# A hybrid SSD/MLA/PEER block on one core: the first norm's statistics taken together, roots on ScalarE, and three U chunks held back

## The chip, the core and the metric

The kernel runs on one core of a Trainium2 chip. A core has five engines that run on their own and wait for each other through semaphores: TensorE (matmuls and transposes, into PSUM), VectorE, ScalarE (activations), GpSimd and SyncE, which here only issues transfers. In profiles they are PE, PEld (PE's weight loads), DVE, ACT, POOL and SP. The metric is device microseconds for one execution. Before the change the median of three runs is 1629.04 us (1628.74 to 1629.06).

## The reference

The input `x` has 512 tokens of 1024 values. What matters here:

```
h   = layer_norm(x, ln_in_g, ln_in_b)                       # the first norm
mix = hybrid_mixer(h, ...)                                  # SSD heads, MLA heads, one output projection
h   = layer_norm(alpha * h + mix, ln_mix_g, ln_mix_b)
ffn = peer(h, w_query, sub_keys, u_table, v_table)          # 8 heads, top 16 of 16384 experts each
out = layer_norm(alpha * h + ffn, ln_ffn_g, ln_ffn_b)       # the last norm

def layer_norm(x, g, b):
    mu  = mean(x);  var = mean((x - mu)**2)
    return (x - mu) * rsqrt(var + 1e-5) * g + b
```

In `peer`, expert e of a token adds g_e * v_e * gelu(u_e . x). All arithmetic is in float32.

## The kernel before

The 512 tokens are four blocks of 128 (`NB` = 4). A float32 matmul is made of three matmuls on split operands (`mm3`, lines 71 to 74): high by high, high by low, low by high. The low part of a weight is its raw value minus its high part. All large weights pass through one stream of 128 x 1024 items (`Stream`, lines 79 to 127): SyncE loads an item into one of three raw buffers (`wir`), ScalarE makes the high part (`wih`, or `wihx` for every fourth item; line 109), VectorE or GpSimd the low part (`wil`, line 119). `get(n)` makes the splits up to item n + `la`, the high parts `ha` items beyond these, and after each split asks for the load that takes the freed raw buffer.

The order of work is written out by hand: each engine runs its instructions in the order in which the program issues them, and so does each transfer queue. In one place, while PEER's routing is prepared, a loop (`drive`, line 1248) weighs planned times of TensorE (`tm[0]`) against those of VectorE (`tm[1]`) and puts in a U chunk whenever TensorE's plan is not ahead.

The parts that the change touches:

First norm (lines 260 to 302). SyncE loads the four blocks of `x` into `XH`, then constants and the first weights. VectorE takes mean and variance of blocks 0 and 1 (`bn_stats`, `bn_aggr`), computes the inverse roots with a bit trick and three Newton steps (`rsqrt`, lines 129 to 139), and ScalarE normalises both blocks. TensorE transposes them, eight pieces each, into eight PSUM banks `PS8`; bank k holds piece k of all four blocks. The same follows for blocks 2 and 3, with the normalising shared by VectorE and ScalarE. Then, per k, ScalarE applies gain and bias (`ht`, and for odd k `HH`), VectorE rounds for even k (`HH`) and makes the low part `HL`. The first two column groups of the input projection (`two`) consume them k by k.

PEER sweeps all experts densely for blocks 0 to 2 (but for the last 16 tokens of block 2) and gathers rows for block 3 and those 16. A U chunk (`u_chunk`) is 24 matmuls for 128 experts over 368 tokens and a Gelu into an `act` tile. `build_g` (line 1097) makes the gate matrix in 48 groups: VectorE builds one-hot matrices (`hot`, lines 1109, 1113, 1114), TensorE multiplies them (lines 1132, 1133), ScalarE copies the result into `stg` (line 1135), and after every fourth group SyncE writes `stg` to memory (lines 1139, 1140). U chunks are put between the groups by `drive` up to `LEAD - RES` = 54 - 2 of them; the other two run after `build_g`. Then SyncE reads the gates back (`gt`, line 1300), VectorE multiplies them with `act` (`P`, line 1323), ScalarE and VectorE split the product (`Ph`, `Pl`, lines 1336, 1343), and from there one U chunk and one V chunk alternate (`v_chunk`, lines 1352 to 1356), until all 128 of each are done; the first of these U chunks still precedes V chunk 0.

Last norm (`ln_out`, line 1472). For each of blocks 0 to 2, VectorE adds the residual, takes the statistics, computes the root in small steps (`norm_chain`, lines 141 to 156) and applies the norm in two halves. Block 2 comes last; its centring (line 1492) is interleaved with the small steps of its root, and its second half is sent out by ScalarE's queue.

Of the kernel before, what the change touches and what calls it, by code (L numbers as in the profile page):

```python
# [11 lines left out]
F32 = mybir.dt.float32  # L12
# [12 lines left out]
D = 1024  # L25
NB = 4
# [9 lines left out]
RES = 2  # L36
# [17 lines left out]
def tile_block(ctx: ExitStack, tc: tile.TileContext, I, out):  # L54
# [85 lines left out]

    def norm_chain(p, mv, tag, out):
# [32 lines left out]

    cs2 = pool("cs2", side="right")
# [84 lines left out]
    V.memset(ones, 1.0)  # L260
    mv4 = lnp.tile([128, NB, 2], F32, name="mv4")
    PS8 = [pa() if k < 4 else pb() for k in range(8)]
    for p in range(2):
        bs = slice(2 * p, 2 * p + 2)
        for b in (2 * p, 2 * p + 1):
            st6 = lnp.tile([128, 2, 6], F32, name="st6", bufs=2)
            for i in range(2):
                V.bn_stats(st6[:, i], XH[:, b, i * 512:(i + 1) * 512])
            V.bn_aggr(mv4[:, b], st6.rearrange("p a b -> p (a b)"))
        ve = lnp.tile([128, 2], F32, name="ve", bufs=2)  # L270
        nm = lnp.tile([128, 2], F32, name="nm", bufs=2)
        V.tensor_scalar(ve, mv4[:, bs, 1], EPS, None, op0=OP.add)
        rs = rsqrt(lnp, ve, [128, 2], "l0")
        V.scalar_tensor_tensor(nm, mv4[:, bs, 0], -1.0, rs, op0=OP.mult, op1=OP.mult)
        for j, cs, act in (((0, slice(0, D), 1), (1, slice(0, D), 1)) if p == 0 else
                           ((0, slice(0, D), 0), (1, slice(0, 512), 1), (1, slice(512, D), 0))):
            t = XH[:, 2 * p + j, cs]
            if act:
                A.activation(t, t, AF.Identity, bias=nm[:, j:j + 1], scale=rs[:, j:j + 1])
            else:  # L280
                V.tensor_scalar(t, t, rs[:, j:j + 1], nm[:, j:j + 1], op0=OP.mult, op1=OP.add)
        for k in range(8):
            for b in (2 * p, 2 * p + 1):
                T.transpose(PS8[k][:, b * 128:(b + 1) * 128], XH[:, b, k * 128:(k + 1) * 128], ident)
        if p == 0:
            win.his(2)
# [1184 lines left out]
    def ln_out(b):  # L1471
# [15 lines left out]
        ch = norm_chain(fin, mv, "lf", o)  # L1487
        for i, _ in enumerate(ch):
            yield
            if b == 2 and i in (2, 4):  # L1490
                cs = ce[i // 2 - 1]
                V.scalar_tensor_tensor(t[:, cs], t[:, cs], mv[:, 0:1], R2[:, 0, cs], op0=OP.subtract, op1=OP.mult)
                yield
# [105 lines left out]
```

## Time and profile before

| | |
|---|---|
| median of three runs | 1629.04 us |
| the profiled execution, its own time | 1627.28 us |
| its span in the profile | 1625.5 us |
| TensorE busy | 1582.6 us, 97% of the span |
| VectorE busy | 1377.3 us, 85% |
| ScalarE busy | 699.8 us, 43% |
| GpSimd busy | 463.3 us, 29% |
| moved by transfers | 393.77 MB, 242 GB/s in the mean |

The profile is one execution seen by the hardware. Its page gives the busy time of each engine, the chain of work that ended last (followed back from the last instruction, at each step to what released it), and the costliest groups of instructions. The trace behind it can be asked for a timeline: one row per instruction or run of equal ones, with its start, its length (of the whole run, if there are several), engine, line, what it writes and reads, and in brackets how long the engine had been idle and what ended that. SPq and ACTq are transfers at the time of their issue. A table of stretches gives busy times, the granted TensorE clock (1.00 is full speed) and the transfer rate of chosen stretches. Matmuls are pipelined: the length of one includes its way through the array, and the spacing of the starts is the pace.

### The profile page before, as it was taken

The page shows a single profiled execution, that of the slowest core. Times are in us where ns is not written, and L with a number is a line of the kernel's source. Part 1 is how long each engine was busy: PE and PEld are TensorE (multiplying, and loading weights), DVE is VectorE, ACT ScalarE, POOL GpSimd, SP SyncE. Part 2 cuts the span into 40 slices and gives each one's busy share as a digit, 9 for nine tenths or more (in the row PEclk, how much of TensorE's full clock was granted, in tenths as well). Part 3 has the DMA queues.
Part 4 walks back from the last instruction along what each step waited for, and adds up shares of the span by engine and source line. Part 5 has one row for each costly group of instructions (what it writes and reads, how often), then busy time and mean ns, then how long its engine had stood idle before and what let it go on. Part 6 is the DMA issues. An engine that isn't in the chain of part 4 may idle for free.

```text
span 1625.5 us, 23770 instructions
## 1 busy us (share of the span) xinstructions
PE 1582.6 (97%) x8640; PEld 1394.3 (86%) x8640; DVE 1377.3 (85%) x2649; ACT 699.8 (43%) x1213; POOL 463.3 (29%) x332
## 2 busy tenths in 40 slices
PE   7999999999999999999899999999999999999997
PEld 5777878888888999998899999999999999888886
DVE  8979688947799999999588788788888888988977
ACT  5575466641433545555433333343333333333341
POOL 0000000000143213200155455555554544533300
PEclk9999999999999999999999999999999999999999
DMA  6242121374432458766799999999999999999973
GB/s 245 91 157 91 46 64 47 103 242 143 135 92 86 123 182 292 285 240 244 251 375 345 339 331 354 344 338 343 329 355 337 344 329 352 360 335 342 335 220 122
DMA packets 150604, 393.77 MB, mean 242 GB/s; under 512 B 12536, under 2 KB 64584, under 8 KB 148696
## 3 DMA queue, kind: packets, MB, share of 16 engines
q1 hardware_dynamic: 107400, 237.76, 43.3%
q0 software_dynamic: 42944, 154.24, 26.2%
q8 instruction: 67, 1.10, 0.3%
q14 instruction: 49, 0.40, 0.1%
q10 hardware_dynamic: 144, 0.26, 0.0%
HBM read 359.66 MB, written 31.51 MB: 241 GB/s over the span
## 4 chain that ended last, share of the span: by engine, by line
PE 74%; DVE 21%; ACT 2%; issue 2%; DMA 1%; DVEq 0%; ACTq 0%; SPq 0%
PE va L1352 10%; PE va L1356 10%; PE va L1353 10%; PE pu L72 8%; PE pu L74 8%; PE pu L73 8%; PE pa L74 3%; PE pa L73 3%; PE pa L72 3%; DVE wil L119 3%; DVE ij L1109 3%; DVE g L1113 2%; DVE t L953 1%; PE pw L73 1%; PE pw L74 1%
## 5 line engine op out<-in xcount | busy, mean ns | idle before, releaser
L109 ACT ACTIVATE wih<-wir 128x1024 fp32r<-128x1024 f32 (+2 forms) x269 | 277.9, 1034 | 264.5 <-DMA wir<-v 90.5
L119 DVE TENSOR_TENSOR wil<-wir,wih 128x1024 fp32r<-128x1024 f32 (+1 forms) x254 | 302.2, 1190 | 103.2 <-ACT wih L109 43.0
L74 PE MATMUL pu<-XTH,wil 128*128 128x368 f32 x1008 | 331.9, 329 | 0.7 <-DVE wil L119 0.7
L72 PE MATMUL pu<-XTH,wih 128*128 128x368 f32 x904 | 299.3, 331 | 0.0
L73 PE MATMUL pu<-XTL,wih 128*128 128x368 f32 x904 | 297.0, 329 | 0.0
L1353 PE MATMUL va<-wil,Ph 128*128 128x512 f32 x726 | 282.7, 389 | 0.0
L1389 POOL DMA_INDIRECT row<-u,ix x128 | 187.6, 1465 | 230.1 <-DVE row L1400 136.7
L1389 POOL DMA_INDIRECT row<-v,ix x128 | 181.3, 1416 | 196.0 <-DVE ac L1406 167.6
L74 PEld LDWEIGHTS pu<-XTH,wil 128*128 128x128 f32 x1008 | 189.3, 188 | 1.3 <-DVE wil L119 1.3
L73 PEld LDWEIGHTS pu<-XTL,wih 128*128 128x128 f32 x904 | 170.0, 188 | 2.9
L72 PEld LDWEIGHTS pu<-XTH,wih 128*128 128x128 f32 x904 | 169.8, 188 | 2.9
L1352 PE MATMUL va<-wih,Ph 128*128 128x512 f32 x432 | 168.5, 390 | 0.0
L1406 DVE SCALAR_TENSOR_TENSOR ac<-row,hd,ac 128x1024 f32<-128x1024 f32 x128 | 164.0, 1281 | 3.0 <-DMA row<-v,ix 0.9
L1353 PEld LDWEIGHTS va<-wil,Ph 128*128 128x128 f32 x726 | 136.3, 188 | 25.9
L1205 ACT ACTIVATE act<-pu 128x368 f32<-128x368 f32 x126 | 59.9, 476 | 221.3 <-PE pu L74 196.3
L1400 DVE SCALAR_TENSOR_TENSOR row<-row,x 128x1024 f32<-128x1024 f32 x128 | 150.1, 1219 | 2.4 <-DMA row<-u,ix 2.4
L109 ACT ACTIVATE wihx<-wir 128x1024 fp32r<-128x1024 f32 x67 | 71.1, 1061 | 158.3 <-DMA wir<-v 129.9
L1356 PE MATMUL va<-wih,Pl 128*128 128x512 f32 x432 | 133.4, 390 | 0.0
L119 DVE TENSOR_TENSOR wil<-wir,wihx 128x1024 fp32r<-128x1024 f32 x62 | 75.9, 1223 | 51.4 <-issue 45.5
L1352 PE MATMUL va<-wihx,Ph 128*128 128x512 f32 x294 | 114.9, 391 | 0.9 <-ACT Ph L1336 0.9
L1356 PEld LDWEIGHTS va<-wih,Pl 128*128 128x128 f32 x432 | 81.1, 188 | 17.2
L1352 PEld LDWEIGHTS va<-wih,Ph 128*128 128x128 f32 x432 | 81.2, 188 | 15.8
(458 smaller groups left out, 3073.7 us busy)
## 6 DMA issues: line engine op xcount, KB each, us to landing
wir<-ut SPq DMA_DIRECT2D x128, 512.0 KB
wir<-v SPq DMA_DIRECT2D x128, 512.0 KB
gsp<-stg SPq DMA_DIRECT2D x12, 1920.0 KB
gt<-gsp SPq DMA_DIRECT2D x30, 768.0 KB
wir<-wo SPq DMA_DIRECT2D x26, 512.0 KB
wir<-wf SPq DMA_DIRECT2D x18, 512.0 KB
wir<-wqr SPq DMA_DIRECT2D x16, 512.0 KB
de<-acd POOLq DMA_DIRECT2D x8, 512.0 KB
```

The costliest lines, as they stand in the source:

```text
L72: T.matmul(ps, lh, rh, start=start, stop=False)
L73: T.matmul(ps, lh, rl, start=False, stop=False)
L74: T.matmul(ps, ll, rh, start=False, stop=stop)
L109: A.activation(h, r, AF.Copy)
L119: self.lo(n).tensor_tensor(l, r, h, op=OP.subtract)
L1205: A.activation(ACT[c][:, :NU], ps, AF.Gelu)
L1352: T.matmul(va[b][e], Ph[:, bs], h[:, cs], start=c == 0, stop=False)
L1353: T.matmul(va[b][e], Ph[:, bs], l[:, cs], start=False, stop=False)
L1356: T.matmul(va[b][e], Pl[:, bs], h[:, cs], start=False, stop=c == 127)
L1389: G.indirect_dma_start(out=R[s], out_offset=None, in_=I["u"] if s < 128 else I["v"], in_offset=bass.IndirectOffsetOnAxis(ap=ix[:, s % 128: ...
L1400: V.scalar_tensor_tensor(r, r, 1.0, x3, op0=OP.mult, op1=OP.mult, accum_out=hd[:, s:s + 1])
L1406: V.scalar_tensor_tensor(ac, r, hd[:, s - 128:s - 127], ac, op0=OP.mult, op1=OP.add)
```

## The change

Three edits.

First norm: the statistics of all four blocks come first, then one chain for all four inverse roots (`sqrt_rs`): ScalarE takes the square root of variance + eps, VectorE its reciprocal and one Newton step. ScalarE normalises block 2, VectorE blocks 0, 1 and 3. The transposes follow in the order 0, 2, 1, 3, and the first two high parts of weights (`win.his(2)`) come after them in the program. A one-element root (`w0`) stands at the start, so that ScalarE's table with the root is loaded there.

Last norm: block 2 uses `sqrt_chain`, the same root in five instructions, with the two centring products between them; blocks 0 and 1 keep `norm_chain`. Two one-element activations before the norm make ScalarE load the table of the root.

U chunks: `RES` is 3, so that `drive` stops one U chunk earlier and three run after `build_g`.

```
-RES = 2
+RES = 3
...
+    def sqrt_rs(p, v, shape, tag):
+        h, q, y, a = (p.tile(shape, F32, name=tag + n) for n in "hqya")
+        A.activation(q, v, AF.Sqrt, bias=eps)
+        V.tensor_scalar(h, v, EPS, -0.5, op0=OP.add, op1=OP.mult)
+        V.reciprocal(y, q)
+        V.tensor_tensor(a, y, y, op=OP.mult)
+        V.tensor_tensor(a, a, h, op=OP.mult)
+        V.scalar_tensor_tensor(y, a, 1.5, y, op0=OP.add, op1=OP.mult)
+        return y
+
+    def sqrt_chain(p, mv, tag, out):
+        h, q, a, y = (p.tile([128, 1], F32, name=tag + n) for n in "hqay")
+        A.activation(q, mv[:, 1:2], AF.Sqrt, bias=eps)
+        V.tensor_scalar(h, mv[:, 1:2], EPS, -0.5, op0=OP.add, op1=OP.mult)
+        yield
+        V.reciprocal(y, q)
+        yield
+        V.scalar_tensor_tensor(a, y, h, y, op0=OP.mult, op1=OP.mult)
+        yield
+        V.scalar_tensor_tensor(y, a, 1.5, y, op0=OP.add, op1=OP.mult)
+        out.append(y)
+        yield
...
     V.memset(ones, 1.0)
+    V.memset(eps, EPS)
     mv4 = lnp.tile([128, NB, 2], F32, name="mv4")
+    w0 = lnp.tile([128, 1], F32, name="w0")
+    A.activation(w0, ones[:, 0:1], AF.Sqrt, bias=eps)
     PS8 = [pa() if k < 4 else pb() for k in range(8)]
-    for p in range(2):
-        bs = slice(2 * p, 2 * p + 2)
-        for b in (2 * p, 2 * p + 1):
-            st6 = lnp.tile([128, 2, 6], F32, name="st6", bufs=2)
-            for i in range(2):
-                V.bn_stats(st6[:, i], XH[:, b, i * 512:(i + 1) * 512])
-            V.bn_aggr(mv4[:, b], st6.rearrange("p a b -> p (a b)"))
-        ve = lnp.tile([128, 2], F32, name="ve", bufs=2)
-        nm = lnp.tile([128, 2], F32, name="nm", bufs=2)
-        V.tensor_scalar(ve, mv4[:, bs, 1], EPS, None, op0=OP.add)
-        rs = rsqrt(lnp, ve, [128, 2], "l0")
-        V.scalar_tensor_tensor(nm, mv4[:, bs, 0], -1.0, rs, op0=OP.mult, op1=OP.mult)
-        for j, cs, act in (((0, slice(0, D), 1), (1, slice(0, D), 1)) if p == 0 else
-                           ((0, slice(0, D), 0), (1, slice(0, 512), 1), (1, slice(512, D), 0))):
-            t = XH[:, 2 * p + j, cs]
-            if act:
-                A.activation(t, t, AF.Identity, bias=nm[:, j:j + 1], scale=rs[:, j:j + 1])
-            else:
-                V.tensor_scalar(t, t, rs[:, j:j + 1], nm[:, j:j + 1], op0=OP.mult, op1=OP.add)
+    for b in range(NB):
+        st6 = lnp.tile([128, 2, 6], F32, name="st6", bufs=2)
+        for i in range(2):
+            V.bn_stats(st6[:, i], XH[:, b, i * 512:(i + 1) * 512])
+        V.bn_aggr(mv4[:, b], st6.rearrange("p a b -> p (a b)"))
+    nm = lnp.tile([128, NB], F32, name="nm")
+    rs = sqrt_rs(lnp, mv4[:, :, 1], [128, NB], "l0")
+    V.scalar_tensor_tensor(nm, mv4[:, :, 0], -1.0, rs, op0=OP.mult, op1=OP.mult)
+    for b in (2, 0, 1, 3):
+        t = XH[:, b]
+        if b == 2:
+            A.activation(t, t, AF.Identity, bias=nm[:, b:b + 1], scale=rs[:, b:b + 1])
+        else:
+            V.tensor_scalar(t, t, rs[:, b:b + 1], nm[:, b:b + 1], op0=OP.mult, op1=OP.add)
+    for b in (0, 2, 1, 3):
         for k in range(8):
-            for b in (2 * p, 2 * p + 1):
-                T.transpose(PS8[k][:, b * 128:(b + 1) * 128], XH[:, b, k * 128:(k + 1) * 128], ident)
-        if p == 0:
-            win.his(2)
+            T.transpose(PS8[k][:, b * 128:(b + 1) * 128], XH[:, b, k * 128:(k + 1) * 128], ident)
+    win.his(2)
     win.splits(1)
...
-        ch = norm_chain(fin, mv, "lf", o)
+        ch = (sqrt_chain if b == 2 else norm_chain)(fin, mv, "ls" if b == 2 else "lf", o)
         for i, _ in enumerate(ch):
             yield
-            if b == 2 and i in (2, 4):
-                cs = ce[i // 2 - 1]
+            if b == 2 and i in (0, 1):
+                cs = ce[i]
                 V.scalar_tensor_tensor(t[:, cs], t[:, cs], mv[:, 0:1], R2[:, 0, cs], op0=OP.subtract, op1=OP.mult)
...
     A.activation(xr[2], xr[2], AF.Copy, scale=ALPHA)
+    w0 = fin.tile([128, 1], F32, name="w0")
+    A.activation(w0, xr[2][:, 0:1], AF.Square)
+    A.activation(w0, w0, AF.Sqrt, bias=eps)
```

`eps` is a small constant tile from a new pool of its own.

2 lines of the change are left out of this document (added).

## The prediction

> **What bounds the kernel now.** I read the page first: the span, the busy shares and the chain of work that ended last.
>
> ```profile
> span 1625.5 us, 23770 instructions
> ...
> PE 74%; DVE 21%; ACT 2%; issue 2%; DMA 1%; DVEq 0%; ACTq 0%; SPq 0%
> ```
>
> TensorE carries 74% of the chain, VectorE 21%. Three short stretches are touched by the change, so the question is who holds TensorE in each of them. I read them in the timeline, in order of time: the first norm, the last groups of `build_g` with the start of the V phase, and the last norm.
>
> The first norm (start, length, engine, line, operation, what ended the idle time):
>
> ```profile
> 4.09 1.29 DVE L268 BATCH_NORM_STATS2 st<-XH 128x6 f32<-128x512 f32 x2 [3.08 <-DMA XH<-x]
> ...
> 7.05 0.17 DVE L272 TENSOR_SCALAR ve<-mv 128x2 f32<-128x2 f32 x1
> ...
> 9.42 0.16 DVE L274 SCALAR_TENSOR_TENSOR nm<-mv,l0y 128x2 f32<-128x2 f32 x1
> ...
> 9.50 1.28 DVE L268 BATCH_NORM_STATS2 st<-XH 128x6 f32<-128x512 f32 x2
> ...
> 9.62 2.37 ACT L279 ACTIVATE XH<-XH,nm,l0y 128x1024 f32<-128x1024 f32 x2 [4.19 <-DVE nm L274]
> ...
> 12.04 1.75 PE L284 MATMUL pa<-ident,XH 128*128 128x128 f32 x7 [0.66 <-ACT XH L279]
> ...
> 14.82 0.16 DVE L274 SCALAR_TENSOR_TENSOR nm<-mv,l0y 128x2 f32<-128x2 f32 x1
> ...
> 15.02 1.27 DVE L281 TENSOR_SCALAR XH<-XH,l0y,nm 128x1024 f32<-128x1024 f32 x2
> ...
> 15.89 1.09 PE L284 MATMUL pa<-ident,XH 128*128 128x128 f32 x8 [0.39 <-DVE XH L281]
> ...
> 16.36 1.45 ACT L291 ACTIVATE ht<-pa,PAR 128x512 f32<-128x512 f32 x2 [0.54 <-PE pa L284]
> ...
> 16.82 1.04 PE L284 MATMUL pb<-ident,XH 128*128 128x128 f32 x8
> ...
> 20.27 0.50 PE L73 MATMUL pa<-HL,wih 128*128 128x512 f32 x1
> ```
>
> VectorE takes the statistics of two blocks, then the small chain (7.05 to 9.42, 13 instructions, 0.2 us each), then the other two blocks and the same chain, and is done with its share of the normalising at 16.29. TensorE transposes blocks 0 and 1 meanwhile, and only the 16 transposes of blocks 2 and 3 are left at 15.89. ScalarE's first `ht` starts at 16.36, two transposes later, because a PSUM bank holds one k of all four blocks. From 20.27 on TensorE has no more idle time in this stage, so what moves that point moves the end.
>
> Two paces of the same transpose stand there: seven in the 1.55 us from 12.04 to 13.59 (where the next row begins), 0.22 us each; eight in the 0.93 us from 15.89 to 16.82, 0.12 us each. The table of stretches (busy time and count of TensorE, its weight loads and the other engines, granted clock, DMA share, GB/s):
>
> ```profile
> 0.00:8.00 8.00, 0.00 (x0) 0.00 (x0) 3.83 (x12) 1.28 (x1) 0.20 (x4) 1.00 0.73 262
> ...
> 12.04:15.43 3.39, 3.39 (x15) 3.06 (x15) 2.87 (x16) 2.25 (x3) 0.00 (x0) 1.00 0.77 282
> ...
> 780.01:783.43 3.42, 1.09 (x16) 0.92 (x16) 3.32 (x5) 1.30 (x3) 0.00 (x0) 1.00 0.41 153
> ...
> 783.43:786.84 3.41, 3.20 (x21) 3.20 (x22) 1.29 (x2) 1.87 (x3) 0.00 (x0) 0.50 0.00 0
> ```
>
> The slow pace holds from 12.04 to 15.43 (15 in 3.39 us), although the clock column says 1.00 there. Later the column does record a clock of 0.50 for 3.41 us, from 783.43, right after a stretch of the same length in which TensorE was busy for 1.09 us of 3.42 (32%). The other rows say that TensorE starts slow and falls back when it idles.
>
> The end of `build_g` and the start of the V phase, and then SyncE's queue over the same time:
>
> ```profile
> 773.04 0.22 PE L1133 MATMUL pw<-g,ij 128*128 128x128 f16 x1
> ...
> 774.61 1.22 DVE L119 TENSOR_TENSOR wil<-wir,wih 128x1024 fp32r<-128x1024 f32 x1
> ...
> 777.17 0.24 PE L1132 MATMUL pw<-ij 128*128 128x128 f16 x1
> ...
> 781.06 0.23 PE L1132 MATMUL pw<-ij 128*128 128x128 f16 x1 [1.50 <-DVE ij L1114]
> ...
> 783.64 0.29 PE L1132 MATMUL pw<-ij 128*128 128x128 f16 x1 [1.49 <-DVE ij L1114]
> ...
> 785.57 0.60 ACT L1135 ACTIVATE stg<-pw 128x512 f32<-128x512 f32 x1 [0.26 <-PE pw L1133]
> ...
> 789.09 0.33 PE L72 MATMUL pu<-XTH,wih 128*128 128x368 f32 x1
> ...
> 797.09 0.33 PE L72 MATMUL pu<-XTH,wih 128*128 128x368 f32 x1
> ...
> 798.62 0.52 ACT L1336 ACTIVATE Ph<-P 128x384 fp32r<-128x384 f32 x1 [3.85 <-DVE P L1323]
> ...
> 799.20 0.50 PE L1352 MATMUL va<-wihx,Ph 128*128 128x512 f32 x1 [0.94 <-ACT Ph L1336]
> ...
> 801.71 1.06 ACT L109 ACTIVATE wih<-wir 128x1024 fp32r<-128x1024 f32 x1 [0.94 <-DMA wir<-v]
> ...
> 802.78 0.46 ACT L1205 ACTIVATE act<-pu 128x368 f32<-128x368 f32 x1
> ```
>
> ```profile
> 775.86 0.33 SPq L91 DMA_DIRECT2D wir<-ut  x1
> ...
> 786.19 0.32 SPq L1139 DMA_DIRECT2D gs<-stg  x1
> ...
> 788.11 3.64 SPq L1300 DMA_DIRECT2D gt<-gs  x2
> ...
> 791.86 4.82 SPq L91 DMA_DIRECT2D wir<-v  x1
> ```
>
> The rows at 773.04 and 777.17 enclose one U chunk; it runs between two of the one-hot groups, of which four follow. VectorE makes a group in 2.58 us (781.06 to 783.64), so TensorE waits for it in the last two. The last staging copy ends at 786.17, then SyncE writes it out, reads `gt` back (the read is issued at 788.11) and issues a weight load at 791.86. Meanwhile TensorE runs three more U chunks (sixteen k-steps in the 8.00 us from 789.09 to 797.09, 4.0 us a chunk), then waits 0.94 us for `Ph`: V chunk 0 starts at 799.20. ScalarE next waits for the weight load that stands behind `gt` in the queue, until 801.71.
>
> **The change part by part.** *First norm.* Gone are 2 chains of 13; in their place stand one root on ScalarE, five dependent small instructions on VectorE and one that runs beside the root. All statistics come first, so the fourth block's landing counts now. By 8.00 the queues had moved 262 GB/s x 8 us, 2.10 MB, which is just the four blocks of 0.52 MB; smaller transfers share the time. VectorE, free of block 1 at 7.0, comes to the fourth at 8.3; I place its landing between there and 9.3 and take 9.0, late in between, because a landing follows its last byte. Statistics until 10.5 (1.28 plus some 0.2 for the aggregate), the root 0.2, by ScalarE's smallest row here,
>
> ```profile
> L1204 ACT ACTIVATE act<-one 128x16 f32<-128x16 f32 x128 | 25.9, 202 | 0.0
> ```
>
> then five times 0.2: normalising begins at 11.8. VectorE's three blocks are done by 14.4 (0.85 each: 1.27 for one and a half), ScalarE's block 2 by 13.0 (1.19, half of 2.37). That is about 2 us sooner than 16.29. But TensorE now starts at 12.7 instead of 10.91, and 25 transposes, not 18, lie ahead of the first `ht`, all after 12.7. At 0.22 us they end at 18.2; if the pace doubles at 15.43 as in this trace, 12.4 are slow and 12.6 fast, until 16.9. Adding the 0.36 us from a transpose's start to `ht` (16.00 to 16.36), `ht` starts at 17.3 to 18.6 where it was 16.36: +0.9 to +2.2 us. With the fourth block at 8.3 the first transpose is at 12.0, the mixed pace ends at 16.6, and the low end is +0.6. The table load only moves ahead of the landing; the weight splits (`his(2)`, `splits(1)`) keep their places behind the normalising and have the time that TensorE spends transposing as cover. I take **+1.2 us**, the mean of the three values +0.6, +0.9 and +2.2.
>
> The Trainium skill speaks against this part: "TensorE: Matmul & The Clock Gate", Part 1, says that the array runs at half rate until a freely running window of about 3.4 us has been busy, so work crowded into the first windows is paid double. The trace agrees in its two paces and its 3.41 us at 0.50; by that rule alone, with the window in its worst place, the sum would be the second rival's.
>
> *Last norm, block 2.* VectorE's rows on this path:
>
> ```profile
> 1617.75 0.14 DVE L145 TENSOR_SCALAR lfh<-fmv 128x1 f32<-128x1 f32 x1
> ...
> 1619.11 0.74 DVE L1492 SCALAR_TENSOR_TENSOR xr<-xr,fmv,R 128x512 f32<-128x512 f32 x1
> ...
> 1619.77 0.21 DVE L152 SCALAR_TENSOR_TENSOR lfa<-lfy,lfh 128x1 f32<-128x1 f32 x1
> ...
> 1620.21 0.22 DVE L152 SCALAR_TENSOR_TENSOR lfa<-lfy,lfh 128x1 f32<-128x1 f32 x1
> ...
> 1620.66 1.41 DVE L1501 SCALAR_TENSOR_TENSOR xr<-xr,lfy,R 128x512 f32<-128x512 f32 x2
> ```
>
> Before, from the slot at 1617.75 on: three small steps, a half-row product, a pair of steps, the second product at 1619.11, two more pairs, and the final pass at 1620.66. After: the first product takes the slot at 1617.75, the reciprocal follows 0.66 later (the spacing of 1619.11 and 1619.77), the second product 0.08 after it, 0.66 later the last pair, 0.45 long (1620.21 to 1620.66): 1617.75 + 0.66 + 0.08 + 0.66 + 0.45 = 1619.60. **-1.06 us**, all on the path, since both output halves follow the final pass. The root (0.2 us) lies beside the first product and has 0.66 us; the table load and two tiny warm-ups stand on ScalarE some 20 us ahead, where it has nothing else to do. If the root were late the gain would shrink by at most its own 0.3 us; the bounds are -0.7 and -1.1.
>
> *Three U chunks held back.* The comparison of the instruction orders shows one U chunk taken from 773.04 and put behind the four groups. VectorE is rid of the 1.22 us split at 774.61, some 1.15 us of its time, since neighbours overlap a little; so the later groups come 1.15 us sooner, the last staging copy ends at 785.0, and `gt` is issued and lands 1.15 us sooner. TensorE, however, ran that chunk under VectorE's group making; now it idles there and has four chunks, 16.0 us, after the last group instead of three. It ends them at 799.5 at full clock, or up to 801.5 if the half clock holds to 786.84 as before; `gt` is no longer late for it.
>
> What is late next is on SyncE and ScalarE. The load that was issued at 775.86, ahead of the last staging writes, is moved behind both `gt` reads, to where the V load of 791.86 stands now. Its ScalarE copy (`wih`) belongs to the chunk three ahead and stands in ScalarE's order before the evacuation of the third held-back chunk and before `Ph` of V chunk 0. So `Ph` waits for a landing that it does not need. That queue position lands at 801.71 now, with the same transfers ahead; 1.15 sooner is 800.56. Then `wih` to evacuation 1.07 (801.71 to 802.78), 0.46 for the evacuation, and 0.58 from `Ph` to the first V matmul (798.62 to 799.20): 802.67 against 799.20, rounded **+3.4 us**. Bounds: if that copy were not in the way, V chunk 0 starts when the chunks end, +0.3; if the last group runs at full clock, half of the 1.7 us or so from 783.64 to its last copy's source is saved, +2.6. Above, +3.9: I allow the 0.5 us that two evacuations could add. I take +3.4, since the slow last group is what the rows show, and TensorE idles more in the new order.
>
> Sum: +1.2 - 1.06 + 3.4 = +3.5 us on the profiled execution, whose own time is 1627.28 (span 1625.5). It was 1.76 us under the median of the runs, 1629.04; the same step on the median gives **1632.5 us**. Behind both places TensorE is the bound, so I count the steps in full.
>
> **The rivals.** *ScalarE does not block* (not slower). Place: the copy ahead of `Ph`. It decides if that load lands before about 798.5, 2 us sooner than its place in the queue says, which could be if it overtakes `gt` on engines that are done sooner. Then the tail costs +0.3 to +2.3 and the total is +0.4 to +2.5: about 1630.5. For it: transfers share engines. Against: the load at 791.86 sat 4.82 us in its issue, behind `gt`.
>
> *The clock falls worse.* All 25 transposes run at the slow pace, one stretch of 3.41 us more than in this trace, and the held-back chunks begin slow: +2.2, +3.4, -1.06, so +4.5, 1633.5. For it: one group is 1.09 us of work in each 2.58, 42%, little over the 32% after which the clock fell. Against: from 12.7 to 15.43 TensorE would be busy for most of a stretch. This is the rule of the skill named above, in its worst phase.
>
> *The chain is shortened and nothing replaces it* (faster). The chain names VectorE in the first norm and `gt` in the tail. With transposes at 0.12 throughout, 25 of them end at 15.7 and `ht` starts at 16.06 (-0.3), or -1.0 with the fourth block at 8.3; the tail gives -1.15 if V chunk 0 follows `gt`; with -1.06 at the end that is -2.5 to -3.2, 1626.2. For the tail it decides from 3.3 us a chunk on (four between 785.0 and 798.05), and the rows say 4.0; so it has little.
>
> **How the numbers follow.** What a measurement of this kernel can tell is about 0.2%, 3.3 us: slower begins at 1632.3. As worked out: 0.49, its own range 1631.0 to 1634.0, a little more of it over the bound (0.33) than under (0.16). ScalarE does not block: 0.18, all within. Clock worse: 0.12, slower. Chain shortened: 0.15, of which 0.10 faster, since 1626.2 is near the lower bound of 1625.8 and its two terms beside the end are the least sure. What I have not seen: 0.06, half of it each way. Slower 0.33 + 0.12 + 0.03 = 0.48, within 0.16 + 0.18 + 0.05 = 0.39, faster 0.13. The range of 8 in 10, 1626.2 to 1634.5, leaves out 0.13 below, the faster part of the third rival and half of the unseen, and some 0.06 above.
>
> **What would show it.** In the changed profile: normalising at about 11.8 and the first `ht` at 17.3 or later; the last staging copy near 785 plus what the front added; TensorE waiting at V chunk 0 for `Ph`, and ScalarE's idle time just before ended by the landing of a `wir` from `ut`; the last final pass 1.06 us closer to its aggregate. It is wrong if `ht` starts before 16.4, or if V chunk 0 follows the last U chunk without a gap.

## The result and the profile after

The changed kernel takes 1639.41 us (median of 6 runs, 1638.62 to 1642.31), the kernel before, beside it on the same chip, 1628.98 us (6 runs, 1627.43 to 1629.41). The ratio is 1.0072, with a 95% interval of 1.0062 to 1.0083: slower by 10.4 us. The forecast was 1632.5 us, slower by 3.5: the sign was right, the size was not, and 1639.4 lies above the range. The profiled execution of the changed kernel took 1642.31 us (span 1640.6), the slowest of its six; the one of before took 1627.28. So the two traces stand 15.0 us apart, more than the medians.

The page of the changed kernel, its head and its chain:

```profile
span 1640.6 us, 23747 instructions
...
PE 1595.9 (97%) x8640; PEld 1404.1 (86%) x8640; DVE 1373.2 (84%) x2625; ACT 700.8 (43%) x1217; POOL 466.1 (28%) x332
...
PE 88%; DVE 9%; ACT 2%; issue 1%; DMA 0%; SPq 0%; DVEq 0%; ACTq 0%
```

TensorE is busy for 13.3 us more (1595.9 against 1582.6) with the same number of matmuls. That is the first hint: the work itself has become slower, beside what waits were added. Both programs issue their matmuls in almost the same order, and both traces hold 8640 of them, so the n-th of one can be set beside the n-th of the other. This table is worked out from the two traces (start in before, and how much later the same matmul starts afterwards, in us):

```
matmul   start before   later by   what lies ahead of it
   400        99.11        1.85     the first norm
  1200       260.77        2.01
  1600       330.60        4.72     a half-clock stretch at 267 us
  4000       723.31        7.59     w_query, early U chunks
  4400       771.31        7.80
  4800       841.21       11.31     end of build_g, chunks held back
  7600      1381.63       15.76     U and V chunks by turns
  8400      1561.10       15.86     V chunks only
```

Two rows of before's timeline and two of the changed kernel's carry the largest item:

```profile
841.21 0.39 PE L1352 MATMUL va<-wih,Ph 128*128 128x512 f32 x1
...
1381.63 0.33 PE L73 MATMUL pu<-XTL,wih 128*128 128x368 f32 x1
```

```profile
852.52 0.39 PE L1374 MATMUL va<-wih,Ph 128*128 128x512 f32 x1
...
1397.40 0.33 PE L73 MATMUL pu<-XTL,wih 128*128 128x368 f32 x1
```

Between these two matmuls stand 540.42 us before and 544.88 us after, in a part of the program that no line of the diff touches. The loss is even, without a step: 0.31 to 0.33 us in every 200 matmuls. Of the 4.45 us, 3.45 lie at the 1600 matmuls of the U chunks and 1.00 at the 1200 of the V chunks between them. It also sits in the projection to the routing (4.72 to 7.59), and it is absent where only V chunks run (15.76 to 15.86). The groups of instructions, before and then after, say which matmuls it is (count, busy us, mean ns of one):

```profile
L74 PE MATMUL pu<-XTH,wil 128*128 128x368 f32 x1008 | 331.9, 329 | 0.7 <-DVE wil L119 0.7
L72 PE MATMUL pu<-XTH,wih 128*128 128x368 f32 x904 | 299.3, 331 | 0.0
L1353 PE MATMUL va<-wil,Ph 128*128 128x512 f32 x726 | 282.7, 389 | 0.0
```

```profile
L74 PE MATMUL pu<-XTH,wil 128*128 128x368 f32 x1008 | 334.2, 332 | 0.0
L72 PE MATMUL pu<-XTH,wih 128*128 128x368 f32 x904 | 301.6, 334 | 0.0
L1375 PE MATMUL va<-wil,Ph 128*128 128x512 f32 x726 | 283.3, 390 | 0.0
```

A U chunk's matmul has become 3 ns longer, a V chunk's has not (1 ns, rounding included). Start to start, in the mean over all of them in each trace, pauses of over 0.3 us left out, it is (ns):

```
                      columns   before   after
w_query   XTH,wih       512      226.7   233.2
          XTH,wil       512      227.4   233.5
          XTL,wih       512      227.5   233.3
U chunk   XTH,wih       368      168.7   172.4
          XTH,wil       368      167.3   168.6
          XTL,wih       368      166.5   167.8
V chunk   wih,Ph        512      227.7   228.3
HH,wih                  512      228.9   228.4
```

What streams `XTH` or `XTL` is slower; in the other rows the pace differs by 0.6 ns at most. In the built programs `XTH` starts at byte 196480 of each partition before and at 196448 afterwards, `XTL` at 212864 and 212832. The new pool `ep` with its four bytes stands ahead of the other pools on that side and moves them down by 32 bytes. The weights' pool is on the other side and stays (`wih` 28800, 32896 and 36992; `wil` 41088, 45184 and 49280).

The three places that the prediction spoke of. The first norm, in the changed kernel's timeline:

```profile
10.80 0.30 ACT L143 ACTIVATE l0q<-mv,eps 128x4 f32<-128x4 f32 x1 [8.46 <-DVE mv L295]
11.13 0.18 DVE L145 RECIPROCAL l0y<-l0q 128x4 f32<-128x4 f32 x1 [0.16 <-ACT l0q L143]
...
12.12 1.24 ACT L302 ACTIVATE XH<-XH,nm,l0y 128x1024 f32<-128x1024 f32 x1 [1.03 <-DVE nm L298]
...
12.99 1.12 PE L307 MATMUL pa<-ident,XH 128*128 128x128 f32 x4 [12.99 <-DVE XH L304]
13.90 1.06 PE L307 MATMUL pb<-ident,XH 128*128 128x128 f32 x4
...
17.31 0.96 PE L307 MATMUL pb<-ident,XH 128*128 128x128 f32 x4
18.11 0.60 PE L307 MATMUL pa<-ident,XH 128*128 128x128 f32 x4
18.42 0.78 ACT L313 ACTIVATE ht<-pa,PAR 128x512 f32<-128x512 f32 x1 [3.16 <-PE pa L307]
```

Normalising begins at 12.12 (forecast 11.8), nearly all of the 25 transposes ahead of the first `ht` run at the slow pace (four in 0.85 us), and `ht` starts at 18.42, 2.06 us later than before; the later matmuls carry 1.85 of it.

The end of `build_g`, and the clock over it:

```profile
790.26 0.29 PE L1154 MATMUL pw<-ij 128*128 128x128 f16 x1 [1.49 <-DVE ij L1136]
792.18 0.60 ACT L1157 ACTIVATE stg<-pw 128x512 f32<-128x512 f32 x1 [0.26 <-PE pw L1155]
...
794.74 3.18 SPq L1322 DMA_DIRECT2D gt<-gs  x2
798.03 4.27 SPq L91 DMA_DIRECT2D wir<-ut  x1
...
808.18 1.06 ACT L109 ACTIVATE wih<-wir 128x1024 fp32r<-128x1024 f32 x1 [5.44 <-DMA wir<-ut]
809.25 0.46 ACT L1227 ACTIVATE act<-pu 128x368 f32<-128x368 f32 x1
809.61 0.51 ACT L1358 ACTIVATE Ph<-P 128x384 fp32r<-128x384 f32 x1
810.18 0.50 PE L1374 MATMUL va<-wihx,Ph 128*128 128x512 f32 x1
```

```profile
786.02:789.44 3.42, 1.26 (x19) 0.92 (x16) 3.32 (x5) 1.91 (x4) 0.00 (x0) 1.00 0.44 184
789.44:792.85 3.41, 2.59 (x19) 2.59 (x20) 1.87 (x3) 1.26 (x3) 0.00 (x0) 0.50 0.00 0
792.85:796.27 3.42, 3.42 (x13) 3.42 (x12) 0.00 (x0) 0.98 (x2) 0.00 (x0) 0.50 0.84 326
796.27:799.68 3.41, 3.41 (x21) 3.41 (x21) 1.22 (x1) 1.47 (x3) 0.00 (x0) 1.00 0.97 289
```

ScalarE does wait, for 5.44 us, for the moved load that now stands behind `gt`, and `Ph` follows its copy. V chunk 0 starts 17.4 us after the last staging copy ends (810.18 less 792.78), 13.0 before. But TensorE has no gap in front of it: the half clock held for two stretches and stretched the four chunks until the same moment.

The last norm of the changed kernel:

```profile
1633.98 0.74 DVE L1514 SCALAR_TENSOR_TENSOR xr<-xr,fmv,R 128x512 f32<-128x512 f32 x1
1634.64 0.16 DVE L156 RECIPROCAL lsy<-lsq 128x1 f32<-128x1 f32 x1
1634.71 0.73 DVE L1514 SCALAR_TENSOR_TENSOR xr<-xr,fmv,R 128x512 f32<-128x512 f32 x1
...
1635.80 1.41 DVE L1523 SCALAR_TENSOR_TENSOR xr<-xr,lsy,R 128x512 f32<-128x512 f32 x2
```

From its slot to the final pass it takes 1.82 us (1635.80 less 1633.98) where it took 2.91 (1620.66 less 1617.75): -1.09.

### The profile page after: what moved, and what is told of

Same layout as the page of the kernel before. It is cut to its first block, busy times and chain, and to the rows that moved or that the text cites. A ratio compares the mean times of both kernels' runs of the same rounds, so it can differ in the third digit from the quotient of the medians.

```text
span 1640.6 us, 23747 instructions
## 1 busy us (share of the span) xinstructions
PE 1595.9 (97%) x8640; PEld 1404.1 (86%) x8640; DVE 1373.2 (84%) x2625; ACT 700.8 (43%) x1217; POOL 466.1 (28%) x332
## 4 chain that ended last, share of the span: by engine, by line
PE 88%; DVE 9%; ACT 2%; issue 1%; DMA 0%; SPq 0%; DVEq 0%; ACTq 0%
PE pu L72 11%; PE pu L74 10%; PE va L1375 10%; PE va L1374 10%; PE va L1378 10%; PE pu L73 10%; PE pw L73 3%; PE pw L74 3%; PE pw L72 3%; PE pa L74 3%; PE pa L72 3%; PE pa L73 3%; DVE ij L1131 2%; DVE wil L119 1%; DVE g L1135 1%; PE pb L514 1%
## 5 line engine op out<-in xcount | busy, mean ns | idle before, releaser
L1411 POOL DMA_INDIRECT row<-v,ix x128 | 184.6, 1442 | 195.3 <-DVE ac L1428 166.2
L1374 PE MATMUL va<-wih,Ph 128*128 128x512 f32 x432 | 168.6, 390 | 0.0
```

The lines of the kernel that those rows point to most:

```text
L1374: T.matmul(va[b][e], Ph[:, bs], h[:, cs], start=c == 0, stop=False)
L1411: G.indirect_dma_start(out=R[s], out_offset=None, in_=I["u"] if s < 128 else I["v"], in_offset=bass.IndirectOffsetOnAxis(ap=ix[:, s % 128: ...
```

## The experiments

Theory at the outset: the three edits cost what was forecast, and the missing part comes from the 32 bytes by which `XTH` and `XTL` moved. Rivals: one of the edits is dearer than forecast, or the loss belongs to the clock. The columns "later by" below are made as in the table above.

**The four bytes alone, and 64 in their place.** The kernel before with the pool and an unused tile; and the changed kernel with the tile 64 bytes wide, so that `XTH` starts 64 bytes lower than before.

```
+    ep = pool("ep", side="right")
+    eps = ep.tile([128, 1], F32, name="eps")
     cs2 = pool("cs2", side="right")
...
+    V.memset(eps, EPS)
```

> The kernel before with one addition: the four-byte tile eps in a pool of its own on the right side of SBUF, filled and never used. In the built program it moves every later right-side tile by 32 bytes; XTH goes from address 196480 (a multiple of 64) to 196448 (32 past one). Theory (place of the moving operand): every matmul that streams XTH or XTL is slower, 227 to about 232 ns at 512 columns and 167 to about 170 at 368, so the program takes about +8 us, 1637, all of it in the two stages that use them (about 390 to 560 and 800 to 1400), none before 390. Rival (the arithmetic and order of the change make the drift, by power or by contention): no difference, 1629.

> The changed kernel with eps made 64 bytes wide instead of 4, so that XTH lies at 196416, a multiple of 64 but not of 128. Theory (place of the operand): about -8 us against the changed kernel, 1631.4, and the pace of the matmuls on XTH back at 227 and 167 ns. If multiples of 128 were needed it stays at 1639. Rival (arithmetic and order): stays at 1639. What is left over the kernel before is then front +1.2 to +2.2, held-back chunk +3, last norm -1.

The tile alone makes it 1637.0 us (4 runs, before 1627.75), ratio 1.0051, interval 1.0035 to 1.0068: about 9 us for a tile that nobody reads. Its matmuls are later by 0.33 at number 1200, 4.56 at 4000, 5.00 at 4800, 9.45 at 7600 and 9.55 at 8400: the even losses of the changed kernel, without its steps in the front and the tail (1.4 of the 4.56 come from a half-clock stretch at 266 us). Its U chunks run at 172.4, 168.6 and 167.8 ns, to the tenth what the changed kernel has. Their first group, here and then in the kernel of the next experiment, in which `XTH` is back in place:

```profile
L72 PE MATMUL pu<-XTH,wih 128*128 128x368 f32 x904 | 302.1, 334 | 0.0
```

```profile
L72 PE MATMUL pu<-XTH,wih 128*128 128x368 f32 x904 | 298.8, 330 | 0.0
```

With 64 bytes the changed kernel stays at 1640.42 (ratio 1.0074, 1.0057 to 1.0091): a start on a multiple of 64 is no cure.

**The tiles put back, and moved by themselves.** In the changed kernel `scl` is allocated ahead of `XTH`, which brings `XTH` back to 196480, while the other pools of that side stay 32 bytes lower; the same edit in the kernel before moves `XTH` up to 196512, `XTL` with it, and no other operand of a matmul.

```
     xt = pool("xt", side="right")
+    scl = xt.tile([128, 1], F32, name="scl")
     XTH = xt.tile([128, 8, S], F32R, name="XTH")
     XTL = xt.tile([128, 8, S], F32R, name="XTL")
     one = xt.tile([128, UG], F32, name="one")
-    scl = xt.tile([128, 1], F32, name="scl")
```

> The changed kernel with one line moved: the 32 bytes of scl are taken ahead of XTH and XTL in their pool, so that XTH is back at 196480 and XTL at 212864 as before, while every other right-side tile stays 32 bytes lower. Theory (place of XTH and XTL alone, to a multiple of 128): the pace on them returns to 218 and 167 ns and the time falls by about 9 us against the changed kernel, to 1630 to 1631. Rival (another shifted tile, or the depth of the right side, makes it): stays at 1639 to 1640.

> The kernel before with the same line moved: XTH and XTL alone go 32 bytes up (196512, 212896), no other operand of a matmul moves and no instruction is added. Theory (place of XTH and XTL): about +8 to +9 us, 1636.5, as in the run with the unused tile. Rival (another tile): no difference, 1628.

The changed kernel with `XTH` back in place takes 1633.35 us (9 runs, before 1628.9), ratio 1.0023, 1.0013 to 1.0033, and its U chunks are back at 168.6, 167.3 and 166.5 ns. Between matmuls 4800 and 7600 it takes the 540.42 us of before, to the hundredth. So 6 of the 10.4 us go with one line that computes nothing, and the rest, +4.4, is left for the three edits and for whatever else the 32 bytes move. The kernel before with `XTH` 32 bytes higher takes 1631.78 (10 runs), ratio 1.002, 1.001 to 1.003: slower, but less than expected, with U chunks at 170.0, 167.1 and 166.8 ns. The same 32 bytes upward cost less than downward, and I had no reason for that. The theory "a streamed tile must start on a multiple of 128 bytes" was shaken.

**Each edit alone.** `RES = 3` in the kernel before; only the last norm; only the first norm (`eps` taken from a pool on the other side, so that nothing moves).

```
-RES = 2
+RES = 3
```

> The kernel before with RES = 3 alone. Theory (load behind gt, ScalarE waits for it ahead of Ph): +3.3 us, 1632.3; ScalarE's copy before Ph waits for the landing of a wir from ut, and V chunk 0 starts 3.3 us later than before counted from the same place. Rival (the chain is only shortened): -1.1, 1627.9. Rival (clock alone): U chunks end late with V chunk 0 right behind, +0.3 to +2.3, and ScalarE's copy has landed before.

> The kernel before with the last norm's root on ScalarE alone (eps in the last pool, which moves no matmul operand). Theory: -1.06 us, 1627.9, with 1.82 us from the slot after the aggregate's first small step to the final pass instead of 2.91. Rival (the root or its table load is late): 0 to -0.7.

> The kernel before with the changed first norm alone (eps in the pool that is released after it, so no later tile moves). Theory (all 32 transposes now lie behind 12.99 us and run at the slow pace): +1.2 to +2.1 us, about 1629.5 with before at 1627.8; the first ht near 18.4. Rival (the chain on VectorE was what held it): -0.5 to -1.5, ht before 16.4.

`RES = 3`: 1631.28 us (10 runs, before 1627.75), ratio 1.0022, 1.0012 to 1.0031: +3.5. The wait stands in its timeline as the prediction had it, `wih` copy, evacuation, `Ph`, V chunk 0, with TensorE waiting 1.15 us:

```profile
791.83 4.31 SPq L91 DMA_DIRECT2D wir<-ut  x1
...
802.45 1.06 ACT L109 ACTIVATE wih<-wir 128x1024 fp32r<-128x1024 f32 x1 [6.64 <-DMA wir<-ut]
...
803.52 0.46 ACT L1205 ACTIVATE act<-pu 128x368 f32<-128x368 f32 x1
803.87 0.51 ACT L1336 ACTIVATE Ph<-P 128x384 fp32r<-128x384 f32 x1
...
804.44 0.50 PE L1352 MATMUL va<-wihx,Ph 128*128 128x512 f32 x1 [1.15 <-ACT Ph L1336]
```

The last norm alone: 1626.21 (10 runs, before 1627.75), ratio 0.9991, 0.9981 to 1.0000; in its trace the half-clock stretch at 783 us is missing, which gives 0.8 of the 1.6 us of its span. The first norm alone: 1628.81 (10 runs, before 1628.9), ratio 1.0005, 0.9995 to 1.0015; `ht` starts at 18.27 and the matmuls behind it are later by 1.73, then by 2.99 after a half-clock stretch at 267 us. In the medians this edit costs less than the +1.2 to +2.1 expected, though `ht` comes as late as expected. None of the three explains more than was forecast. Their medians add up to +1.9 us (3.5 less 1.5 less 0.1), against the +4.4 of the changed kernel with `XTH` in place; the intervals of the four are wide enough for both, and no run shows whether the edits simply add.

**Is the slow pace of the transposes the clock?** The first norm with 16 transposes of the identity ahead of the real ones, into a bank that is overwritten.

```
+    for k in range(16):
+        T.transpose(PS8[7][:, 0:128], ident, ident)
     for b in range(NB):
```

> The same, with 16 idle transposes of the identity into the last PSUM bank (overwritten later) put ahead, which TensorE can run from about 9.5 us, when the identity has landed. Theory (the pace is the clock, which rises after TensorE has been busy for a while): the real transposes run at 0.11 to 0.12 us, or at least more of them do, and the first ht comes at 16 to 17.5: 0.5 to 2 us faster than the first norm alone. Rival (the pace belongs to these transposes, by their operands): no gain.

```profile
9.44 3.67 PE L278 MATMUL pb<-ident 128*128 128x128 f32 x16 [9.44 <-DMA ident<-idn]
...
13.86 0.90 PE L295 MATMUL pb<-ident,XH 128*128 128x128 f32 x4
14.60 0.60 PE L295 MATMUL pa<-ident,XH 128*128 128x128 f32 x4
15.04 0.60 PE L295 MATMUL pb<-ident,XH 128*128 128x128 f32 x4
...
16.66 0.78 ACT L301 ACTIVATE ht<-pa,PAR 128x512 f32<-128x512 f32 x1 [1.42 <-PE pa L295]
```

The idle ones run at 0.22 us, the real ones from 14.60 on at 0.11 (four in 0.44), and `ht` starts at 16.66 instead of 18.27. The trace's own record of the clock has the first full clock at 14.46 here and at 18.10 with the first norm alone. Its place varies from run to run, but in both kernels with idle transposes it came earlier (14.46, and 12.93 in the last experiment) than in all eleven without (15.43 to 18.80). It is the clock: what is put into TensorE's first microseconds is paid double, and work that is there to warm it can take that time. The run is 1627.73 us (10 runs, ratio 0.9994, 0.9984 to 1.0004), no measurable gain over before.

**What in the tail is the wait, what the chunks?** Three chunks held back, but the moved load is issued ahead of the last staging writes; and the size turned the other way, one chunk held back.

```
-RES = 2
+RES = 3
...
-            tm[0] += 1.1
+            tm[0] += 1.1; n == 45 and win.splits(win.ns + 1)
```

> Before with three chunks held back, but the load that went behind gt is issued ahead of the last staging writes, by a split made between the last two groups but one. Tells what of the tail's +3.4 is the wait of ScalarE for that load, and what the four chunks behind the last group by themselves. If the chunks alone set it: ScalarE waits no more for a wir from ut ahead of the first Ph, and V chunk 0 follows the fourth chunk within 0.3 us, some 16 us after the last staging copy; the tail keeps +2.5 to +3.3. If the wait was the cost: V chunk 0 comes back to within 1 us of before's place.

> Before with one U chunk held back instead of two (RES=1), the same knob turned the other way. By the chain of the tail: one more split of 1.15 us on VectorE ahead of the last groups, so the last staging copy and gt come 1.15 us later, and V chunk 0 waits for its P, as it did by 0.94 in before: +1.1 (0.07%), no difference to speak of. If what counts is only the number of chunks behind the last group (4 us each): -3 to -4.

```profile
803.45 0.33 PE L74 MATMUL pu<-XTH,wil 128*128 128x368 f32 x1
803.61 0.39 PE L1352 MATMUL va<-wihx,Ph 128*128 128x512 f32 x1
```

With the load early (one run, 1631.63 us), ScalarE no longer waits ahead of `Ph` and V chunk 0 follows the fourth chunk directly; from matmul 4400 to 4800 it loses 2.68 us against before (1.65 to 4.33), where plain `RES = 3` loses 3.63 (1.62 to 5.25). So in these two executions the wait is worth about 1.0 us and the fourth chunk behind the last group 2.7. One chunk held back gives 1629.64 (10 runs, before 1628.9), ratio 1.0011, 1.0002 to 1.0021, near the +1.1 expected, though not for its reason: V chunk 0 starts at 799.46, 0.26 later than before, but TensorE is idle for a whole stretch ahead of V chunk 0 and the next one is at half clock.

```profile
795.79:799.20 3.41, 0.00 (x0) 0.00 (x0) 0.56 (x1) 0.31 (x1) 0.00 (x0) 1.00 1.19 299
799.20:802.61 3.41, 3.15 (x7) 2.48 (x8) 2.58 (x4) 2.31 (x6) 0.00 (x0) 0.50 0.58 193
```

**The price of an address by itself.** Two kernels of streaming alone, which compute nothing of the reference and ran once each. In the first, TensorE streams one tile from 0 to 128 bytes past its start, or loads the weights from 32 to 96 bytes past theirs.

```
+        run(lambda p, l, k: T.matmul(p[:, 0:512], l, mv[:, k % 3, 0:512], start=k == 0, stop=k == 15))
+        run(lambda p, l, k: T.matmul(p[:, 0:512], l, mv[:, k % 3, 8:520], start=k == 0, stop=k == 15))
...
+        run(lambda p, l, k: T.matmul(p[:, 0:512], l, mv[:, k % 3, 0:512], start=k == 0, stop=k == 15), 8)
```

> The disputed price by itself: nothing of the reference is computed, x is copied out; TensorE streams the same fp32r tile 192 matmuls at a time, 512 columns wide and then 368, each reading from 0, 32, 64, 96 and 128 bytes past a multiple of 128, and then with the stationary operand 32, 64 and 96 bytes past it; all of it twice. If the start of the moving operand is the cause: about 227 ns at 0 and 128 bytes and about 232 at 32, 64 and 96 for 512 columns, 1 to 4 ns more for 368 columns too, and the stationary operand's start changes nothing. If the cause is something else that the new tile shifted with it (the weights, the PSUM side, a neighbour in memory): all eight variants the same within 0.5 ns.

Start to start, at 512 columns: 226.7 ns at no shift, 233.3, 229.0, 233.4 and 233.3 with the streamed tile at 32, 64, 96 and 128 bytes, and 233.3, 233.3 and 234.2 with the weights at 32, 64 and 96. Both of its passes give the same figures. That felled the theory in two places: 128 bytes is as slow as 32, and the weights, which I had expected to be innocent, cost the same. At 368 columns it has 166.7 at no shift, 166.7, 166.7, 173.3 and 165.6 with the streamed tile moved, and 168.9, 168.9 and 166.7 with the weights. The second kernel therefore uses the addresses and the order of a U chunk and moves one, the other, or both.

```
+                x = [mv[:, o + k * 512:o + k * 512 + n] for o in (136 + dm // 4, 4232 + dm // 4)]
+                w = [wt[:, o + k * 128:o + k * 128 + 128] for o in (128 + c % 3 * 1024 + dw // 4, 3200 + c % 3 * 1024 + dw // 4)]
...
+    run(512, 0, 0, lambda p, l, x, s, e: T.matmul(p, l, x, start=s, stop=e))
+    run(512, -32, 0, lambda p, l, x, s, e: T.matmul(p, l, x, start=s, stop=e))
```

> Nothing of the reference is computed, x is copied out. TensorE runs the mixed order of U chunks (wih with XTH, wih with XTL, wil with XTH, over eight k) from tiles at the addresses of before (weights at 28800 and on, XTH at 196480, XTL at 212864), at 512 and 368 columns, with the streamed tiles, the weights, or both moved by 32 to 512 bytes. At no shift: 218 to 221 ns and 166 to 169, as in before's trace; streamed tiles at -32 (the changed kernel): 223 to 226 and 168 to 172. Theory 1, only the streamed tile's address counts: moving the weights alone changes nothing, and moving both by the same is as slow as moving the streamed tile. Theory 2, what counts is how far the two tiles that are read at once stand apart: moving both by the same restores the pace of no shift, and the weights alone by -32 are as slow as the streamed tile by +32. Theory 3, each tile's own start counts against a multiple of 64 or 128: both moved is slowest of all, and -128, -256 are as fast as no shift.

Its groups, one line of the kernel for each case; at 512 columns L88 is no shift, L89 the streamed tiles at -32, L96 the weights at -32, L101 both; at 368 columns L105, L106 and L118 are no shift, the streamed tiles and both:

```profile
L88 PE MATMUL p<-mv,wt 128*128 128x512 f32 x96 | 21.9, 389 | 0.0
...
L89 PE MATMUL p<-mv,wt 128*128 128x512 f32 x96 | 22.6, 396 | 0.0
...
L96 PE MATMUL p<-mv,wt 128*128 128x512 f32 x96 | 22.6, 395 | 0.0
...
L101 PE MATMUL p<-mv,wt 128*128 128x512 f32 x96 | 22.0, 389 | 0.0
...
L105 PE MATMUL p<-mv,wt 128*128 128x368 f32 x96 | 16.2, 329 | 0.0
...
L106 PE MATMUL p<-mv,wt 128*128 128x368 f32 x96 | 16.4, 330 | 0.0
...
L118 PE MATMUL p<-mv,wt 128*128 128x368 f32 x96 | 16.2, 328 | 0.0
```

Start to start, worked out from its trace (ns; the streamed tiles' shift less the weights' in the first column):

```
distance   by                        512 columns   368 columns
    0      none                         226.7         166.7
    0      both by -32                  227.0         166.6
    0      both by -64                  227.0         166.7
    0      both by -96                  227.0         166.6
    0      both by -128                 227.0         166.7
  -32      streamed -32                 233.4         168.8
  -64      streamed -64                 233.2         168.9
  -96      streamed -96                 234.3         166.7
 -128      streamed -128                232.4         173.3
 -256      streamed -256                226.9         166.6
 -512      streamed -512                226.7         166.7
  +32      streamed +32                 233.3         167.8
  +32      weights -32                  233.3         167.8
  +64      weights -64                  228.9         166.7
  +96      weights -96                  233.3         168.8
 +128      weights -128                 233.3         165.6
 +256      weights -256                 227.0         166.7
```

(The 218 to 221 ns expected at no shift were means over all that reads these tiles in the routing stage, two U chunks of 368 columns among them.) Theory 2 holds in this kernel, and at 512 columns in both. What counts is how far the streamed tile and the weights stand apart: both moved alike is as fast as none moved, streamed +32 is the same as weights -32, and distances of 256 and 512 are as good as 0. The unshifted distance is itself a multiple of 256 bytes in both kernels (12288 in the first, 196480 less 28800 in the second). The odd asymmetry above gets its direction: at 368 columns -32 costs 2.1 ns and +32 only 1.1. In the U chunks of the whole kernels it was 2.1 and 0.5 in the mean, so +32 is cheaper there than here.

At 368 columns the distance is not the whole of it: +32 and +96 give 167.8 and 168.8 here, but gave 166.7 and 173.3 in the first kernel, which takes its operands in another order. What makes that difference was not tried.

**The edits that pay, together.** The kernel before with the changed first norm, the 16 idle transposes and the changed last norm, `eps` on the other side, two chunks held back.

> Before, with the changed first norm and 16 idle transposes ahead of it, and the changed last norm; the four bytes of eps taken from the pools lnp and fin, so that XTH stays at 196480, and two U chunks held back as before. If the three edits add up as they did alone: front +0.3 (ht 16.66 for 16.36, or -1 where the half clock near 227 us falls well), end -1.1, nothing between: 1625.5 to 1628, against 1628.9 for before. If the two norms did not add (a root in one slowing the other, tables loaded twice), it would be no faster than either alone, 1626.2 and 1627.7.

It takes 1627.75 us (11 runs, before 1628.9 over 21), ratio 0.9994, 0.9985 to 1.0003: inside the 1625.5 to 1628 expected, faster than the changed kernel, not distinguishable from the kernel before.

## Why the prediction was right or wrong

*The step that failed* is one that the prediction does not name: the four-byte tile `eps` in a pool of its own, which it costed at nothing by leaving it out of "the change part by part". Its place in memory moves `XTH` and `XTL` by 32 bytes against the weights. From the second streaming kernel: 128 U chunks of 24 matmuls by 2.1 ns are 6.5 us, and 16 `w_query` steps of 24 by 6.7 are 2.6, together up to 9.0. The trace of the changed kernel shows 7.3 (2.87 from matmul 1600 to 4000, 4.45 from 4800 to 7600), part of the loss being hidden, as I read it, where VectorE is the limit: the 984 matmuls of U chunks between 1600 and 4000 lose only 0.84. The runs show 6 (taken back) to 9 (put in alone). With this term the forecast would have been +9.5 to +12.5; +10.4 was measured.

The Trainium skill, "SBUF — State Buffer", section "SBUF: two separate sides", says of TensorE's reads that they never wait on anyone, and its section "A bandwidth-pool intuition that's wrong (but worth ruling out)" gives the weight load an independent read port. The runs show something else, and they decide: 226.7 or 233.4 ns for the same two reads at 512 columns, by their distance alone.

*First norm*, forecast +1.2 within +0.6 to +2.2: 1.85 in the trace, 1.73 in the trace of this edit alone. By the medians this edit alone is -0.1 (-0.8 to +2.4), so the time itself shows neither the loss nor its absence. In the traces the mechanism was right. Two sizes were off: normalising began at 12.12 rather than 11.8 (the root began at 10.80, not 10.5, after VectorE had waited 0.81 us for the third block and none for the fourth, and it takes 0.30 us, not 0.2), and the full clock came at 18.03, not 15.43, so that the value at the slow end was the true one.

*Last norm*, forecast -1.06: -1.09 by the rows.

*Held-back chunk*, forecast +3.4 (its own terms add up to 3.47): +3.5 from matmul 4400 to 4800 in the changed kernel, 3.63 with this edit alone, and +3.5 by that edit's medians (+2.0 to +5.0). The size was right, the reason only in part, so the agreement is in part luck. The wait of ScalarE for the moved load is there, row by row, but it is worth only 1.0 us; 2.7 us are the fourth chunk itself behind slow last groups. For the case without the wait the prediction had +0.3 to +2.3, with the half clock until 786.84 at the latest; where the load was early it held until 788.22. In the changed kernel the wait is even hidden, because the half clock held for 6.83 us: V chunk 0 follows the last U chunk without a gap, which the prediction had named as a sign of being wrong.

*The sum* of the three, +3.5, stands against +4.4 us by the medians with `XTH` in place (ratio 1.0013 to 1.0033, that is +2.1 to +5.4), and +4.1 by that run's span (1629.6 against 1625.5). The forecast of these parts is within what was measured.

*The clock between the stages* is a term of the traces alone that no step has. The half-clock stretch that before's trace has at 227 us lies at 265 to 268 us in eight of the twelve other traces of the kernel and its variants, the changed kernel's among them, and costs between matmuls 1200 and 1600 1.2 to 1.5 us there, and 2.7 in the changed kernel, where it lasts 6.83 us. The first norm alone has it at 267, the last norm alone at 226, the changed kernel with `XTH` in place at 228: nothing shown here ties it to the change. What differs is how TensorE's work falls into the clock's stretches of 3.41 us: before, the one from 223.64 has TensorE busy for 1.35 us and the half clock follows; in the changed kernel the one from 226.23 has 1.93 and the full clock stays, until one from 263.79 with 1.83. The stretch makes a good part of the 4.6 us by which the two profiled executions stand further apart than the medians.

*The rivals.* "The clock falls worse" came true in the front (nearly all transposes slow) and, in the profiled execution, in the tail (6.83 us at half clock): 0.7 us above the forecast in the one place, 0.1 in the other, so it is not the miss. Its total of +4.5 lies nearer than the forecast to the +4.4 with `XTH` in place, but that interval holds both. "ScalarE does not block" falls with the row at 802.45, and "the chain is shortened" with `ht` at 18.42 and V chunk 0 at 810.18.

## What to carry to other kernels

A tile that computes nothing can cost more than all the computing it serves: after any edit that allocates, compare the addresses of the large tiles in the built program with those before, and keep the streamed operand and the weights of a hot matmul a multiple of 256 bytes apart, the distances that cost nothing at either width here. When a change makes a kernel slower, set the same instruction of both traces side by side along the whole program; steps are waits or a slow clock, and an even slope is a price per instruction, in a place that the diff may not mention.

## What the runs showed of the hardware

The pace of a matmul with fp32r operands depends on the distance in memory between what it streams and the weights it loads. At 512 columns it is 226.7 to 227.0 ns where the distance is changed by 0, 256 or 512 bytes, 228.9 to 234.3 in all other cases. At 368 columns the same distances give 166.6 to 166.7, others from 165.6 to 173.3, with a sign: 128 bytes lower is the slowest case and 128 higher the fastest (in the first streaming kernel 96 higher was as slow, 173.3). Why these values and not others stays open, as does whether other types behave so.

The half clock comes in stretches of 3.41 us and their multiples (6.83 and 10.24 were seen), with a phase of its own: the first full clock came between 12.93 and 18.80 us after the start, from run to run. In each of the thirteen traces of the whole kernel and its variants all changes of the clock lie whole numbers of 3.413 us apart (15.43 and 227.05 before: 62 of them). This agrees with the Trainium skill, "TensorE: Matmul & The Clock Gate", Part 1, which describes a freely running window of 3.413 us. Where that page speaks of an idle window, a window that was busy for 1.26 us of 3.42, in short pieces, was enough here (the row at 786.02). On that grid, in the thirteen traces, each of the 35 stretches at full clock in which TensorE was busy for up to half was followed by half clock; of those above half only one was, at 1.83 us of 3.41.
